# A streaming log-softmax backward kernel: 128-row tiles in 32 KiB runs become 256-row groups with 64 KiB runs and a new store order

## The chip, the cores and the metric

The kernel runs on one core of a Trainium2 chip. The metric is the device time of one execution in microseconds (us), taken as the median over several executions. The executions were made on several chips. The kernel before was run beside each experiment, and its medians on four of these chips were 1871.6, 1871.72, 1871.8 and 1871.83 us. The chips therefore differ by about 0.2 us. A profile is of one execution; its trace holds the instructions and the DMA packets. The span of a profile is 1.7 to 2.0 us shorter than the time of the execution that it shows.

A DMA moves data between DRAM and SBUF, the core's working memory, which is laid out in 128 partitions. PSUM is a second memory of the core. 16 DMA engines share the work of each DMA in the profiles here. They move it as packets: a run of 32 KiB, that is 32 KiB that lie in one piece in both memories, is one packet. At the end of a DMA each engine leaves one small packet more, its completion record. A buffer is the space for one tile.

## The reference, cut to what matters

```python
# y, dy: float32 [8, 1024, 8192]
softmax_x = np.exp(y)
sum_dy = np.sum(dy, axis=-1, keepdims=True)
return dy - softmax_x * sum_dy          # float32
```

There are 8,192 rows of 8,192 numbers. The row sum needs all of a dy row before the first output of that row can be made. Two arrays are read and one is written, 268.4 MB each, 805.3 MB in all. No change to the kernel can lessen that.

## The kernel before

A tile holds 128 rows, one row (32 KiB) per partition. For each tile the kernel loads dy, loads y, sums dy on the vector engine (DVE), takes exp on the scalar engine (ACT) into PSUM, and computes dy - sum * exp in place on DVE, 2,048 columns at a time. Three tiles are computed and then stored together. All DMAs are issued from the sync engine's queue (SP).

```python
def subtract_scaled_exp(nc, psum, y_part, dy_part, neg_sum, width):   # width = 2048
    for c in range(0, y_part.shape[-1], width):
        e_t = psum.tile([128, width], fp32)
        nc.scalar.activation(e_t[:], y_part[:, c : c + width], ACT_EXP)
        nc.vector.scalar_tensor_tensor(out=dy_part[:, c : c + width], in0=e_t[:],
            scalar=neg_sum, in1=dy_part[:, c : c + width], op0=ALU.mult, op1=ALU.add)
# dyp: BATCH + 1 = 4 buffers, yp: 2 buffers
for b, e in zip(starts, starts[1:] + [n_tiles]):          # BATCH = 3 tiles
    done = []
    for i in range(b, e):
        sl = ts(i, P)
        nc.sync.dma_start(out=dy_t[:], in_=dy_f[sl])       # [128, 8192]
        nc.sync.dma_start(out=y_t[:], in_=y_f[sl])
        nc.vector.tensor_reduce(out=s_t[:], in_=dy_t[:], axis=X, op=ALU.add, negate=True)
        subtract_scaled_exp(nc, psum, y_t, dy_t, s_t[:], CD)
        done.append((sl, dy_t))
    for sl, dy_t in done:
        nc.sync.dma_start(out=out_f[sl], in_=dy_t[:])
# ... allocation lines cut
```

## Time and profile before

| | kernel before |
|---|---|
| time, median | 1871.77 us (3 runs, 1871.63 to 1871.79) |
| span of the profile | 1870.2 us |
| bytes moved, mean rate | 805 MB, 431 GB/s |
| DVE, ACT busy | 61%, 26% |

The first excerpt is from the page of the kernel before: busy time per engine, the share of busy DMA in 40 slices of the span, the rate in the same slices, the packets, the DMA queue, the chain that ended last, and the three costly groups of instructions (busy us, mean ns of one, then the engine's idle time in front of them and what ended it).

```profile
DVE 1136.0 (61%) x320; ACT 477.5 (26%) x257; POOL 0.2 (0%) x4
...
DMA  9999999999999999999999999999999999999998
GB/s 404 437 428 435 429 435 431 433 435 429 435 430 435 432 432 435 429 435 430 434 434 430 436 429 433 433 432 435 431 433 432 432 435 430 435 430 434 434 432 383
DMA packets 27656, 805.38 MB, mean 431 GB/s; under 512 B 3072, under 2 KB 3072, under 8 KB 3072
...
q1 hardware_dynamic: 27648, 805.32, 100.0%
...
DMA 61%; DVE 13%; ACT 5%; SPq 1%; issue 0%; DVEq 0%; ACTq 0%
...
L69 DVE TENSOR_REDUCE s_t<-dy_t 128x1 f32<-128x8192 f32 x64 | 555.4, 8679 | 576.0 <-DMA dy_t<-in_dy_dram 576.0
L19 ACT ACTIVATE e_t<-y_t 128x2048 f32<-128x2048 f32 x256 | 476.3, 1877 | 1370.6 <-DMA y_t<-in_y_dram 1295.5
L20 DVE SCALAR_TENSOR_TENSOR dy_t<-e_t,s_t,dy_t 128x2048 f32<-128x2048 f32 x256 | 584.0, 2344 | 139.5 <-ACT e_t L19 139.5
```

Read it from the DMA rows. The 16 DMA engines are busy in every slice, and their queue fills 100.0% of the span. The compute engines wait for loads. The chain that ended last gives DVE 13% and ACT 5%, but this only says who waited for whom at each step; a gain on DVE would come to nothing while the DMA stays full. 3,072 of the 27,656 packets are completion records (16 per DMA, 192 DMAs) and 24,576 are 32 KiB each.

### The profile page before, as it was taken

The numbers are of one execution on the slowest core, as the hardware profiler recorded it, in microseconds if no ns is written. First come the engines' busy times: TensorE is split into PE (matmuls) and PEld (weight loads), VectorE is DVE, ScalarE is ACT, GpSimd is POOL, SyncE is SP. The second block draws the span as 40 slices with busy tenths as digits, with TensorE's granted clock in tenths as the row PEclk, the third lists the DMA queues.
The fourth block names the chain that finished last, engine by engine and source line by source line (L and its number), as shares of the span: only waits on it lengthen the run. The fifth ranks groups of instructions, "written<-read, shape, count | busy, mean of one in ns | idle before, by whom it ended". The sixth has DMA issues, their size and how long they took to land.

```text
span 1870.2 us, 1067 instructions
## 1 busy us (share of the span) xinstructions
DVE 1136.0 (61%) x320; ACT 477.5 (26%) x257; POOL 0.2 (0%) x4
## 2 busy tenths in 40 slices
DVE  6738384756657383839384755647383839374655
ACT  2214131313223131314131313223131414131322
POOL 0000000000000000000000000000000000000000
DMA  9999999999999999999999999999999999999998
GB/s 404 437 428 435 429 435 431 433 435 429 435 430 435 432 432 435 429 435 430 434 434 430 436 429 433 433 432 435 431 433 432 432 435 430 435 430 434 434 432 383
DMA packets 27656, 805.38 MB, mean 431 GB/s; under 512 B 3072, under 2 KB 3072, under 8 KB 3072
## 3 DMA queue, kind: packets, MB, share of 16 engines
q1 hardware_dynamic: 27648, 805.32, 100.0%
q14 instruction: 8, 0.07, 0.0%
HBM read 536.87 MB, written 268.44 MB: 431 GB/s over the span
## 4 chain that ended last, share of the span: by engine, by line
DMA 61%; DVE 13%; ACT 5%; SPq 1%; issue 0%; DVEq 0%; ACTq 0%
DMA y_t<-in_y_dram 61%; DVE dy_t L20 13%; ACT e_t L19 5%; SPq L65 1%; SPq L75 0%; DVEq L101 0%; ACTq L19 0%; SPq L67 0%
## 5 line engine op out<-in xcount | busy, mean ns | idle before, releaser
L69 DVE TENSOR_REDUCE s_t<-dy_t 128x1 f32<-128x8192 f32 x64 | 555.4, 8679 | 576.0 <-DMA dy_t<-in_dy_dram 576.0
L19 ACT ACTIVATE e_t<-y_t 128x2048 f32<-128x2048 f32 x256 | 476.3, 1877 | 1370.6 <-DMA y_t<-in_y_dram 1295.5
L20 DVE SCALAR_TENSOR_TENSOR dy_t<-e_t,s_t,dy_t 128x2048 f32<-128x2048 f32 x256 | 584.0, 2344 | 139.5 <-ACT e_t L19 139.5
L19 ACT ACT_TABLE_LOAD x1 | 1.3, 1283 | 0.7 <-PEq L90 0.7
L90 POOL MEMSET const-bfloat16-1.0<- 128x1 bf16 x1 | 0.1, 102 | 0.0
L90 POOL MEMSET const-uint8-127<- 128x1 uint8 x1 | 0.1, 102 | 0.0
L90 POOL MEMSET const-float32-0.0<- 128x1 f32 x1 | 0.1, 99 | 0.2 <-issue 0.2
L90 POOL MEMSET const-float32-1.0<- 128x1 f32 x1 | 0.1, 99 | 0.0
## 6 DMA issues: line engine op xcount, KB each, us to landing
dy_t<-in_dy_dram SPq DMA_DIRECT2D x64, 4096.0 KB, 45.2
y_t<-in_y_dram SPq DMA_DIRECT2D x64, 4096.0 KB, 36.3
out_dram<-dy_t SPq DMA_DIRECT2D x64, 4096.0 KB, 27.7
```

Source lines behind the costliest of these rows:

```text
L19: nc.scalar.activation(e_t[:], y_part[:, c : c + width], ACT_EXP)
L20: nc.vector.scalar_tensor_tensor(out=dy_part[:, c : c + width], in0=e_t[:], scalar=neg_sum, in1=dy_part[:, c : c + width], op0=ALU.mult, o ...
L65: nc.sync.dma_start(out=dy_t[:], in_=dy_f[sl])
L69: nc.vector.tensor_reduce(out=s_t[:], in_=dy_t[:], axis=mybir.AxisListType.X, op=ALU.add, negate=True)
L90: nc = _bacc.Bacc("TRN2", target_bir_lowering=False, num_devices=1)
```

## The change: its intent and its diff

A group is now 256 rows with two neighbouring rows per partition. For dy and out these two rows are contiguous in DRAM and in SBUF, so a run is 64 KiB long instead of 32. y stays at 32 KiB. Two 64 KiB y buffers beside two of dy would take 256 KiB in each partition, where the tiles of both kernels take 192. The number of DMAs falls from 192 to 129. exp now overwrites y in SBUF (no PSUM), 4,096 columns at a time. Each store is queued behind the dy load of the following group, and the last store but one is held back behind the last y loads.

```diff
-    CD = 2048
-    BATCH = 3
+    R = 2
+    G = N // (P * R)
+    CD = D // 2
+    dy_v = dy.flatten_outer_dims().rearrange("(g p r) d -> g p (r d)", p=P, r=R)   # y, out alike
-    dyp = ... bufs=BATCH + 1      yp = ... bufs=2      psum = ... bufs=2
+    dyp = ... bufs=2              yp = ... bufs=R
+    def load_dy(g):
+        dy_t = dyp.tile([P, R * D], fp32, name="dy_t")
+        nc.sync.dma_start(out=dy_t[:], in_=dy_v[g])
+        nc.vector.tensor_reduce(out=s_t[:], in_=dy_t[:].rearrange("p (r d) -> p r d", r=R), ...)
+    def load_y(g):                    # R loads of one row per partition
+        nc.sync.dma_start(out=y_t[:], in_=y_v[g][:, r * D : (r + 1) * D])
+    def compute(dy_t, s_t, y_ts):     # for r in range(R), for c in range(0, D, CD)
+                nc.scalar.activation(e, e, EXP)
+                nc.vector.scalar_tensor_tensor(out=d, in0=e, scalar=s_t[:, r : r + 1], in1=d, ...)
+    cur = load_dy(0)
+    for g in range(G):
+        if g < G - 1:
+            y_ts = load_y(g)
+            compute(*cur, y_ts)
+            nxt = load_dy(g + 1)
+            if g < G - 2:
+                store(g, cur[0])
+                cur = nxt
+            else:
+                held, cur = cur, nxt
+        else:
+            y_ts = load_y(g)
+            compute(*cur, y_ts)
+            store(g - 1, held[0])
+            store(g, cur[0], parts=R)
# ... cut: the removed helper and loop shown above, the body of store()
```

More of the change, by code (lines that the diff above doesn't have):

```diff
@@ L7 @@
 from concourse.bass import ts
-ACT_EXP = mybir.ActivationFunctionType.Exp
+EXP = mybir.ActivationFunctionType.Exp
 ALU = mybir.AluOpType
-def subtract_scaled_exp(nc, psum, y_part, dy_part, neg_sum, width):
-    total = y_part.shape[-1]
-    for c in range(0, total, width):
-        e_t = psum.tile([128, width], mybir.dt.float32, name="e_t")
-        nc.scalar.activation(e_t[:], y_part[:, c : c + width], ACT_EXP)
-        nc.vector.scalar_tensor_tensor(
-            out=dy_part[:, c : c + width],
-            in0=e_t[:],
-            scalar=neg_sum,
-            in1=dy_part[:, c : c + width],
-            op0=ALU.mult,
-            op1=ALU.add,
-        )
 @with_exitstack
@@ L42 @@
     fp32 = mybir.dt.float32
-    y_f = y.flatten_outer_dims()
-    dy_f = dy.flatten_outer_dims()
-    out_f = out.flatten_outer_dims()
-    N, D = y_f.shape
-    n_tiles = N // P
-    assert N == n_tiles * P
-    CD = 2048
-    BATCH = 3
-    dyp = ctx.enter_context(tc.tile_pool(name="dyp", bufs=BATCH + 1))
-    yp = ctx.enter_context(tc.tile_pool(name="yp", bufs=2))
-    psum = ctx.enter_context(tc.tile_pool(name="psum", bufs=2, space=bass.MemoryType.PSUM))
-    stats = ctx.enter_context(tc.tile_pool(name="stats", bufs=8))
@@ L58 @@
-    first = n_tiles % BATCH
-    starts = [0] * bool(first) + list(range(first, n_tiles, BATCH))
-    for b, e in zip(starts, starts[1:] + [n_tiles]):
-        done = []
-        for i in range(b, e):
-            sl = ts(i, P)
-            dy_t = dyp.tile([P, D], fp32, name="dy_t")
-            nc.sync.dma_start(out=dy_t[:], in_=dy_f[sl])
-            y_t = yp.tile([P, D], fp32, name="y_t")
-            nc.sync.dma_start(out=y_t[:], in_=y_f[sl])
-            s_t = stats.tile([P, 1], fp32, name="s_t")
-            nc.vector.tensor_reduce(
-                out=s_t[:], in_=dy_t[:], axis=mybir.AxisListType.X, op=ALU.add, negate=True
-            )
-            subtract_scaled_exp(nc, psum, y_t, dy_t, s_t[:], CD)
-            done.append((sl, dy_t))
-        for sl, dy_t in done:
-            nc.sync.dma_start(out=out_f[sl], in_=dy_t[:])
+    N, D = y.flatten_outer_dims().shape
@@ new lines @@
+    R = 2
+    G = N // (P * R)
+    assert N == G * P * R
+    CD = D // 2
+    y_v = y.flatten_outer_dims().rearrange("(g p r) d -> g p (r d)", p=P, r=R)
+    dy_v = dy.flatten_outer_dims().rearrange("(g p r) d -> g p (r d)", p=P, r=R)
+    out_v = out.flatten_outer_dims().rearrange("(g p r) d -> g p (r d)", p=P, r=R)
+    dyp = ctx.enter_context(tc.tile_pool(name="dyp", bufs=2))
+    yp = ctx.enter_context(tc.tile_pool(name="yp", bufs=R))
+    stats = ctx.enter_context(tc.tile_pool(name="stats", bufs=2))
@@ new lines, in load_dy @@
+    def load_dy(g):
+        dy_t = dyp.tile([P, R * D], fp32, name="dy_t")
+        nc.sync.dma_start(out=dy_t[:], in_=dy_v[g])
+        s_t = stats.tile([P, R], fp32, name="s_t")
+        nc.vector.tensor_reduce(
+            out=s_t[:],
+            in_=dy_t[:].rearrange("p (r d) -> p r d", r=R),
+            axis=mybir.AxisListType.X,
+            op=ALU.add,
+            negate=True,
+        )
+        return dy_t, s_t
+    def load_y(g):
+        y_ts = []
+        for r in range(R):
+            y_t = yp.tile([P, D], fp32, name="y_t")
+            nc.sync.dma_start(out=y_t[:], in_=y_v[g][:, r * D : (r + 1) * D])
+            y_ts.append(y_t)
+        return y_ts
@@ new lines, in compute, with store @@
+    def compute(dy_t, s_t, y_ts):
+        for r in range(R):
+            for c in range(0, D, CD):
+                e = y_ts[r][:, c : c + CD]
+                d = dy_t[:, r * D + c : r * D + c + CD]
+                nc.scalar.activation(e, e, EXP)
+                nc.vector.scalar_tensor_tensor(
+                    out=d, in0=e, scalar=s_t[:, r : r + 1], in1=d, op0=ALU.mult, op1=ALU.add
+                )
+    def store(g, dy_t, parts=1):
+        w = R * D // parts
+        for k in range(parts):
+            nc.sync.dma_start(
+                out=out_v[g][:, k * w : (k + 1) * w], in_=dy_t[:, k * w : (k + 1) * w]
+            )
```

## The prediction

> **What bounds the kernel now.** The page of the kernel before shows the DMA engines at nine tenths or more in nearly every slice; one queue takes 100.0% of the 16 engines' span, 805 MB at 431 GB/s. DVE is busy 61%, ACT 26%. The chain that ended last names y loads (61%). The trace's packet records say what the DMA time is made of: 24,576 packets of 32 KiB, 1,213 ns at the median; all packets over 16 engines make 1,867.7 us of the 1,870.2 us span (1,215.9 ns each, 1,536 an engine). There is almost no DMA idle time to win; only the cost per byte or packet can fall.
>
> **What the change does to that.** The bytes stay. The Trainium skill, page "DMA: Bandwidth & Descriptors", section "Where 436 GB/s comes from", gives 16 x 32 B x 850 MHz = 435.2 GB/s as ceiling: 1,204.7 ns for 32 KiB, 1,850.5 us for all. The trace agrees within 1%: 1,213 ns, 8 to 11 ns per packet over it. I estimate that this excess is fixed per packet. dy and out go to 64 KiB packets, y stays: 1,024 packets an engine. 512 x 8 to 11 ns saves 4 to 6 us. If the excess is per byte, or 64 KiB runs are split, nothing. Fewer completions (129 DMAs, not 192; 9 ns a record): under 1 us.
>
> **What moves.** Per 256-row group the DMA has about 58 us (three transfers of 19.4). DVE needs two row sums (8.68 us each now) and four scaled adds of 4,096 (2.28 us per 2,048 now, so about 4.5 each): 35 us. ACT: 14. Both fit. Critical is the store: behind the last y half[...] come an exp of 4,096 (3.6 us), two scaled adds (9), issue and first byte (1.7): about 16 us. The next dy load, queued in front of that store, feeds the DMA for 19.4 us: 3 us of slack, no bubble. The dy load after that waits for the older store to complete, but has two y loads (19.4 us) in front. y buffers are now freed by DVE, not ACT (exp in place), yet their loads sit behind the store that waits for the same work: nothing lost. At the start, dy, row sums and adds take about 58 us against 60 us of queued loads: 0 to 1.5 us lost. At the end the last compute hides under the held-back store; the tail stays.
>
> **Prediction.** 1871.8 - 4.5 + 0.5, rounded: 1867.5 us, range 1860 to 1875. Faster by over 2%: 0.01 (the ceiling is 1.1% away). Within 2%: 0.94. Slower by over 2%: 0.05.
>
> **What would show it.** About 18,600 DMA packets, not 27,656; a 64 KiB packet near 2,418 to 2,424 ns; 432 to 433 GB/s; no slice under 425 except first and last; DVE and ACT busy nearly as before (1,136 and 470 us); in the DMA queue's waits, stores waiting for scaled adds while the DMA stays full.
>
> **What would make it wrong.** Packets split, nothing gained (1872). The 3 us of slack eaten by slower SBUF operands or by DMA engines that drift apart: then each of 32 groups gets a bubble, and 1 us each costs 32 us. y rows 64 KiB apart meeting a slower HBM pattern, seen as 32 KiB packets over 1,213 ns.

One clause is cut from it: a figure of 2 us for the landing of data after its last packet. No trace shows it; those of the two kernels show 0.3 to 0.5 us.

## The result, and the profile after

The changed kernel took 1867.83 us (median of 6 runs, 1867.19 to 1872.63) against 1871.68 us (median of 6). The ratio of its runs to those of the kernel before is 0.9986, with a 95% interval of 0.9973 to 0.9999: the same within 2%, but just clear of 1. A ratio here is the mean time of one kernel's runs over that of the other's in the same rounds, so it is not quite the ratio of the medians. The prediction was 1867.5 us.

The same parts of the page for the changed kernel:

```profile
DVE 1119.2 (60%) x160; ACT 457.1 (25%) x129; POOL 0.2 (0%) x4
...
DMA  9999999999999999999999999999999999999999
GB/s 427 416 434 431 443 433 422 435 437 436 427 433 431 440 430 434 431 429 441 433 437 425 433 442 431 434 425 436 438 434 433 428 434 437 437 431 430 429 435 396
DMA packets 18582, 805.36 MB, mean 432 GB/s; under 512 B 2064, under 2 KB 2064, under 8 KB 2064
...
q1 hardware_dynamic: 18576, 805.31, 99.9%
...
DMA 74%; DVE 17%; ACT 6%; SPq 1%; issue 1%; DVEq 0%; ACTq 0%
...
L70 DVE SCALAR_TENSOR_TENSOR dy_t<-y_t,s_t,dy_t 128x4096 f32<-128x4096 f32 x128 | 568.1, 4481 | 490.3 <-ACT y_t L69 490.1
L69 ACT ACTIVATE y_t<-y_t 128x4096 f32<-128x4096 f32 x128 | 455.9, 3608 | 1375.6 <-DMA y_t<-in_y_dram 1375.6
L47 DVE TENSOR_REDUCE s_t<-dy_t 128x2 f32<-128x16384 f32 x32 | 551.0, 17220 | 232.1 <-DMA dy_t<-in_dy_dram 232.1
```

The DMA is still full; there are a third fewer packets. Nothing else that matters has moved. The DVE wait in front of the scaled adds grew from 139.5 to 490.3 us at no cost, because DVE is not the bottleneck. In the DMA queue's own waits, the stores wait for the scaled adds, as predicted, for 985.9 us in all, while the DMA stays full:

```profile
SPq L77 <- DVE dy_t L70: 985.9, 32, 35.0
```

The slices of the rate jump more than before (416 to 443) because the view books a packet's bytes in the slice in which it starts. With the bytes spread evenly over each packet's duration, all slices but the first and the last lie between 430 and 434 GB/s.

Next is the timeline of the changed kernel for one group (start us, duration us, instruction, and the idle time before it), which shows the store order at work.

```profile
149.38 7.12 ACT L69 ACTIVATE y_t<-y_t 128x4096 f32<-128x4096 f32 x2 [41.51 <-DMA y_t<-in_y_dram]
...
159.10 7.12 ACT L69 ACTIVATE y_t<-y_t 128x4096 f32<-128x4096 f32 x2 [2.59 <-DMA y_t<-in_y_dram]
162.75 8.88 DVE L70 SCALAR_TENSOR_TENSOR dy_t<-y_t,s_t,dy_t 128x4096 f32<-128x4096 f32 x2 [0.83 <-ACT y_t L69]
171.66 0.34 SPq L77 DMA_DIRECT2D out_dram<-dy_t  x1
172.09 0.86 SPq L60 DMA_DIRECT2D y_t<-in_y_dram  x2
178.45 17.22 DVE L47 TENSOR_REDUCE s_t<-dy_t 128x2 f32<-128x16384 f32 x1 [6.83 <-DMA dy_t<-in_dy_dram]
```

The second y half's last packet ended at 158.62 us (from the packet records), and exp began at 159.10: the data counted as landed 0.5 us after its last packet. The store was issued at 171.66. The first DMA of the kernel was issued at 0.73 and its first packet is at 1.74, so a store's first packet can start about 1 us after its issue, here at about 172.7. The 16 engines do not finish the dy load in front of it together: the first is done at 176.97 and the last at 178.06. The store was ready about 5.3 us before the last engine needed it, but only 4.3 us before the first did. This margin is called the slack below.

The packet records of the traces say where the 4.8 us between the two spans went. (The two profiled executions took 1872.19 and 1867.19 us, 5.0 us apart, where the medians are 3.9 us apart. So up to about 1 us of what follows may belong to these two executions and not to the kernels.) In this table "sum" is the duration of all packet records over 16 engines. "Overlap" is the time in which more than 16 records were open, over 16: an engine opens the next record a little before the last one closes. (The records do not name their engine. They can be chained into 16 rows by letting each record follow one that it overlaps by a few ns; within such a row the overlap is 3.5 ns a record.) "Mean finish" and "last finish" are the ends of the 16 engines' last completion records. "Slow" is what packets over 30 ns above their median took beyond it, over 16. All are us, finishes from the start of the span.

```
kernel      packets   median ns of    sum      overlap  mean    last    slow
            an engine 32 KiB  64 KiB                    finish  finish
before        1536    1213      -     1869.39    6.06   1865.48 1868.97  1.89
changed       1032    1213    2418    1864.28    4.14   1862.16 1864.20  2.57
difference    -504                      -5.11   -1.92     -3.32   -4.77
```

A 64 KiB packet takes 2,418 ns where two of 32 KiB took 2,426. The 504 packets saved per engine take 504 x 8 = 4.0 us out of the records, 63 fewer completions of 9 ns about 0.6 us, and small items the rest of the 5.1 us. But 1.9 us of that had been overlapped before and was no time at all. What is left, 3.2 us, is what the mean finish shows (3.3 us). The last 1.4 us are at the end: in the kernel before, the slowest engine finished 3.5 us behind the mean, in the changed one 2.0 us.

### The profile page after: what moved, and what is told of

Same layout as the page of the kernel before. It is cut to its first block, busy times and chain, and to the rows that moved or that the text cites. A ratio compares the mean times of both kernels' runs of the same rounds, so it can differ in the third digit from the quotient of the medians. Undisturbed runs are those within 1.5% of the kernel's fastest.

```text
span 1865.4 us, 712 instructions
## 1 busy us (share of the span) xinstructions
DVE 1119.2 (60%) x160; ACT 457.1 (25%) x129; POOL 0.2 (0%) x4
## 2 busy tenths in 40 slices
DMA packets 18582, 805.36 MB, mean 432 GB/s; under 512 B 2064, under 2 KB 2064, under 8 KB 2064
## 4 chain that ended last, share of the span: by engine, by line
DMA 74%; DVE 17%; ACT 6%; SPq 1%; issue 1%; DVEq 0%; ACTq 0%
DMA y_t<-in_y_dram 69%; DVE dy_t L70 15%; ACT y_t L69 6%; DMA dy_t<-in_dy_dram 3%; DVE s_t L47 2%; DMA out_dram<-dy_t 1%; SPq L60 1%; SPq L77 1%; DVEq L122 0%; ACTq L69 0%; DVEq L70 0%
## 5 line engine op out<-in xcount | busy, mean ns | idle before, releaser
L70 DVE SCALAR_TENSOR_TENSOR dy_t<-y_t,s_t,dy_t 128x4096 f32<-128x4096 f32 x128 | 568.1, 4481 | 490.3 <-ACT y_t L69 490.1
L69 ACT ACTIVATE y_t<-y_t 128x4096 f32<-128x4096 f32 x128 | 455.9, 3608 | 1375.6 <-DMA y_t<-in_y_dram 1375.6
L47 DVE TENSOR_REDUCE s_t<-dy_t 128x2 f32<-128x16384 f32 x32 | 551.0, 17220 | 232.1 <-DMA dy_t<-in_dy_dram 232.1
```

The source lines that it names most:

```text
L47: nc.vector.tensor_reduce(out=s_t[:], in_=dy_t[:].rearrange("p (r d) -> p r d", r=R), axis=mybir.AxisListType.X, op=ALU.add, negate=True,)
L69: nc.scalar.activation(e, e, EXP)
L70: nc.vector.scalar_tensor_tensor(out=d, in0=e, scalar=s_t[:, r : r + 1], in1=d, op0=ALU.mult, op1=ALU.add)
```

## The experiments

Theory A, the prediction's: each packet carries a fixed cost of about 8 ns whatever its size, so longer runs of bytes are the gain, and the rest (order of stores, exp in place) only has to keep the DMA fed. Rival B: the gain is from fewer DMAs or from spreading the stores, not from run length. Rival C: the cost is per byte and the gain is chance. All edits are to the changed kernel; all results were correct.

### The changed kernel unedited, as the baseline

> The changed kernel, unedited, as the baseline on this chip. All theories: about 1867.5 us, 3 to 5 us under the kernel before. The first six runs ranged from 1867.2 to 1872.6, so single runs near 1872 may come again; their share is what this run is also for.

Measured: 1867.3 us (5 runs, 1866.79 to 1871.63), ratio 0.9982 (0.9969 to 0.9994). The gain repeats. One execution of five was at 1871.63 us.

### 32 KiB packets with the same DMAs

```diff
-        dy_t = dyp.tile([P, R * D], fp32, name="dy_t")
-        nc.sync.dma_start(out=dy_t[:], in_=dy_v[g])
+        dy_t = dyp.tile([P, R, D + 16], fp32, name="dy_t")
+        nc.sync.dma_start(out=dy_t[:, :, :D], in_=dy_v[g].rearrange("p (r d) -> p r d", r=R))
# row sums, adds and stores address dy_t[:, r, ...] accordingly
```

> Same DMAs, same order, same sizes as the changed kernel, but a 64-byte gap between the two rows in SBUF forces 32 KiB packets. Theory A (a fixed cost of about 8 ns per packet): 1,544 packets an engine instead of 1,032, packets back at 1,213 ns, so +4 us: about 1871.5 us, level with the kernel before. Rival B (the gain comes from fewer DMAs or from the new order of stores): stays at about 1867.5 us. Rival C (per-byte cost, gain from fewer slow packets by luck): no clear difference from the changed kernel.

Measured: 1871.32 us (1869.19 to 1876.59, 5 runs), ratio to the kernel before 1.0003 (0.999 to 1.0015). This line of its page shows the packets (24,576 of 32 KiB and, as in the changed kernel, 2,064 completions in 129 DMAs, besides 6 of the instruction queue):

```profile
DMA packets 26646, 805.36 MB, mean 430 GB/s; under 512 B 2064, under 2 KB 2064, under 8 KB 2064
```

The number of DMAs, their order and their bytes are those of the changed kernel, and the gain is gone. That speaks for A and against B. The five executions scatter, though (1869.19 to 1876.59 us), so the next experiment was needed.

### 32 KiB packets by one DMA per row

```diff
-        nc.sync.dma_start(out=dy_t[:], in_=dy_v[g])
+        for r in range(R):
+            nc.sync.dma_start(out=dy_t[:, r * D : (r + 1) * D], in_=dy_v[g][:, r * D : (r + 1) * D])
-    def store(g, dy_t, parts=1):
+    def store(g, dy_t, parts=R):
```

> The changed kernel with dy and out moved as two 4 MiB DMAs each, one per row of the pair: 32 KiB packets and 192 DMAs, as many as before, in the new order. Theory A: about 1871.5 to 1872 us; against the padded variant only 63 more completions, under 1 us. Rival B, number of DMAs: clearly slower than the padded variant. Rival B, order of stores: about 1867.5 us.

Measured: 1871.29 us (1870.82 to 1871.86, 5 runs), ratio to the kernel before 0.9999 (0.9986 to 1.0011). With the new order, exp in place and large groups, but with the old packets and the old number of DMAs, the kernel is level with the one before. Its page has the packets of the kernel before:

```profile
DMA packets 27655, 805.38 MB, mean 431 GB/s; under 512 B 3072, under 2 KB 3072, under 8 KB 3072
```

The intervals of the two ratios overlap, so the difference rests on the single executions: 13 of 16 of the changed kernel, over its three sets, lie between 1866.79 and 1868.23 us, and all five of this one between 1870.82 and 1871.86. It is also level with the padded variant, so 63 completions more or less do not show in the medians. The length of the runs of bytes carries the gain.

### 16 KiB and 8 KiB packets

```diff
-        dy_t = dyp.tile([P, R * D], fp32, name="dy_t")
+        dy_t = dyp.tile([P, R * S, W + 16], fp32, name="dy_t")     # S = 2 or 4, W = D // S
-            y_t = yp.tile([P, D], fp32, name="y_t")
+            y_t = yp.tile([P, S, W + 16], fp32, name="y_t")
```

> All three tensors in 16 KiB packets, same DMAs and order as the changed kernel: 3,072 packets an engine. Theory A: 2,040 more packets an engine at 8 ns is +16 us, about 1884 us, with packets of about 611 ns at the median. Per-byte rival: unchanged, about 1868 us, packets of 606 ns.

> All three tensors in 8 KiB packets: 6,144 an engine. Theory A: 5,100 more packets an engine than the changed kernel at 8 ns is +41 us, about 1908 us, packets of about 309 ns. Per-byte rival: about 1868 us.

Measured: 1876.7 us (1876.27 to 1877.53, 4 runs) and 1893.73 us (1893.14 to 1894.08, 4 runs). Both are slower, so the per-byte rival C is out. But the size is a miss: +9.4 and +26.4 us over the changed kernel where 8 ns a packet gave +16 and +41. The packet records explain it:

```
kernel      packets   median ns   sum      overlap  mean    last
            an engine one packet                    finish  finish
one DMA/row   1536      1213     1869.22    6.06   1865.21 1868.81
16 KiB        3072       611     1881.69   12.30   1871.85 1873.62
8 KiB         6144       309     1906.21   20.17   1888.47 1890.57
```

The records' excess did behave as expected (611 and 309 ns). The overlap grows along with the number of packets, at 3.3 to 4.0 ns each, and that part is never paid. In mean finish, with 9 ns per completion taken off, a further packet costs (1871.85 - 1865.21 + 0.57) / 1536 = 4.7 ns from 32 to 16 KiB, 5.4 ns from 16 to 8 KiB, and (1865.21 - 1861.85 - 0.57) / 504 = 5.5 ns from 64 to 32 KiB (1861.85 us is the baseline run's mean finish). These are differences of single profiles, and they depend on which ones are taken. The padded variants start their first packet 0.4 us later, which makes the first figure 4.4 ns. The padded 32 KiB variant would give 9.3 ns for the last step with the same correction, but its profiled execution (1873.6 us, above its median) had 2.7 us more of slow packets than the baseline's; without these it gives 4.0. Taken from the medians of the executions instead, with the end of the kernel in them, the three steps are 3.9, 5.5 and 6.8 ns. So a fixed cost is real at all these sizes, and about 5 ns by the records' mean finish; the 8 ns of the records alone are not what a packet costs. At 16 and 8 KiB no run separates the padding from the packet size; at 32 KiB the padded variant and the one without padding are level. The Trainium skill, page "DMA: Bandwidth & Descriptors", section "Why small descriptors are slow (HBM only)", speaks of a fixed overhead of about 3 cycles per packet. If these are cycles of the 850 MHz in its neighbouring section, which the page does not say, an estimate is 3.5 ns. The runs here show about 5 ns (4.4 to 5.5), the same order, and show it at packets of up to 64 KiB, where the page's example is 256 bytes. That it is the same overhead is not shown.

### How much slack the store order leaves

```diff
# at the end of compute(), after the group's last scaled add; n = 1 or 3
+        for _ in range(n):
+            nc.vector.tensor_scalar(out=d, in0=d, scalar1=1.0, scalar2=None, op0=ALU.mult)
```

> One more pass over the last 4,096 columns (times 1.0, about 2.2 us on the vector engine) before each group's store. The trace of the changed kernel puts the store's first packet about 5 us before the end of the dy load queued in front of it (the prediction said 3). Both figures: the delay fits in the slack, no change, about 1867.5 us. If the DMA queue has no real slack: 31 x 2.2 = +68 us.

> Three such passes, about 6.6 us per group. Slack of 5.2 us, as read from the trace: a bubble of about 1.4 us in each of 31 groups, about 1910 us. Slack of 3 us, as predicted: 3.6 us each, about 1980 us. If the slack is far larger than read: no change.

Measured: 1879.11 us (1876.3 to 1880.64, 5 runs) with one pass and 1952.19 us (1952.0 to 1952.43, 4 runs) with three. Both numbers are misses: no change and about 1910 us were expected. (They are compared with the 1867.3 us of the changed kernel on another chip; on this one only the kernel before was run beside them, at 1871.72 us.) The timelines of the two, one pass first, show one group each:

```profile
396.75 8.88 DVE L70 SCALAR_TENSOR_TENSOR dy_t<-y_t,s_t,dy_t 128x4096 f32<-128x4096 f32 x2 [0.83 <-ACT y_t L69]
405.67 2.29 DVE L74 TENSOR_SCALAR dy_t<-dy_t 128x4096 f32<-128x4096 f32 x1
407.99 0.34 SPq L79 DMA_DIRECT2D out_dram<-dy_t  x1
...
412.40 17.22 DVE L47 TENSOR_REDUCE s_t<-dy_t 128x2 f32<-128x16384 f32 x1 [4.43 <-DMA dy_t<-in_dy_dram]
```

```profile
361.86 6.95 DVE L74 TENSOR_SCALAR dy_t<-dy_t 128x4096 f32<-128x4096 f32 x3
368.83 0.34 SPq L79 DMA_DIRECT2D out_dram<-dy_t  x1
369.27 1.34 SPq L60 DMA_DIRECT2D y_t<-in_y_dram  x2
369.38 17.22 DVE L47 TENSOR_REDUCE s_t<-dy_t 128x2 f32<-128x16384 f32 x1 [0.57 <-DMA dy_t<-in_dy_dram]
```

With three passes, 6.95 us are added, and the packet records have no packet at all open for 48.4 us, 1.56 us per group over 31 groups. 6.95 - 1.56 = 5.4 us: with the engines in step, as they are in this run, the slack is what the trace showed for the last engine. What the expectation lacked is the price of a queue that ran empty. Packets over 30 ns above their median took 29.4 us an engine in all, 27 us more than in the changed kernel, or 0.9 us per restart, and engines starting and stopping apart took the rest of the 85 us. These slow packets are mostly one per engine and group: the last packet of a store (23 of the 29.4 us).

With one pass the DMA as a whole was never empty before the end, though 14 of the 16 engines ran dry for up to 0.64 us each in front of the first store. Slow packets took 11.4 us instead of 2.6, 7.7 of them in the second half of the span, which is the 9 us by which that profiled execution was longer. The packet records of the 21st store (us after the store's issue) show both runs beside the changed kernel:

```
kernel        dy load in front of it ends    last packets of the     their mean excess
              first engine    last engine    store start             over 2,418 ns
changed           2.85            6.25       19.76 .. 23.15             0 ns
one pass          1.52            4.50       18.42 .. 21.40           267 ns
three passes     -1.18           -0.75       17.84 .. 18.00           754 ns
```

The engines drift apart. The completion records of one DMA lie 0.7 us apart at the start of the changed kernel and 3.4 us apart late in it. So the first engine's slack shrinks: the store's data can flow about 1 us after its issue, which leaves that engine 1.9 us at the 21st store, where the last one has 5.3. One pass of 2.3 us is more than 1.9. This fits the time lost before the 5.2 us read from the trace are used up, though with one pass the engines seldom ran dry: what cost the time was the slow packets.

It would be natural to blame the slow packets on engines in step, as they are after an empty queue. The traces do not bear this out. In the one-pass run the second to fourth stores end with all 16 engines within 0.9 us of one another, and the slow packets there are 0.02 us an engine or less; the 2,048-column variant below is as close together at the same stores and has none. What goes with the slow packets is the first engine's margin. Over the first 30 stores of six profiles (three of the changed kernel, the 2,048-column variant and the two delayed runs), the slow packets at a store's end were under 0.05 us an engine in all 130 stores where the first engine finished the dy load 2 us or more after the store's issue. They were 0.2 to 0.5 us in the last 16 of these stores of the one-pass run, where that time was 0.7 to 1.6 us, also in those where the engines were 2 us and more apart. This is something that goes together in the traces; no run was made to separate it. Why the loss falls on the last packet of the store, some 20 us later, stays open.

### y in 64 KiB packets too

```diff
-    yp = ctx.enter_context(tc.tile_pool(name="yp", bufs=R))
+    yp = ctx.enter_context(tc.tile_pool(name="yp", bufs=1))
+        y_t = yp.tile([P, R * D], fp32, name="y_t")
+        nc.sync.dma_start(out=y_t[:], in_=y_v[g])          # one load per group
```

> y as well in 64 KiB packets: one 8 MiB load per group into one buffer. Theory A: 256 fewer packets an engine, 2 us less packet time, 64 KiB packets at 2,418 ns. But the chain behind the y landing grows to 0.5 + 3.6 + 17.7 + 1.0 = 22.8 us against 19.35 us of dy load in front of the store: about 3.5 us of bubble in 31 groups, so about 1970 to 1975 us.

Measured: 2004.43 us (2 runs). There are 256 packets an engine fewer, but the chain behind the y landing no longer fits under the dy load: no packet is open for 102.2 us, 3.3 us per group (3.5 expected), and slow packets take another 27 us, as in the delayed run. This is why the change leaves y at 32 KiB. The expectation was short by the cost of the restarts.

### The store in front of the dy load: a first attempt that did not do it

```diff
-            nxt = load_dy(g + 1)
-            if g < G - 2: ...          # and the held-back store at the end
+            store(g, cur[0])
+            cur = load_dy(g + 1)
```

> One part undone: each store is queued in front of the next group's dy load (all 64 KiB runs stay). If the order is what keeps the DMA fed, the queue now blocks on the scaled adds with nothing behind the y load: from the last y packet to the first store packet about 17 us per group (dy landing, 17.2 us of row sums, 17.7 us of adds, 1 us of issue, less 19.4 us of y load), about 2410 us. If the order doesn't matter: 1867.5 us.

Measured: 1876.03 us (2 runs, 1873.93 and 1878.12), which would say that the order hardly matters. The timeline tells otherwise:

```profile
346.16 0.34 SPq L77 DMA_DIRECT2D out_dram<-dy_t  x1
346.59 0.86 SPq L60 DMA_DIRECT2D y_t<-in_y_dram  x2
...
372.58 0.33 SPq L45 DMA_DIRECT2D dy_t<-in_dy_dram  x1
...
404.58 0.34 SPq L77 DMA_DIRECT2D out_dram<-dy_t  x1
```

The dy load is still issued before the store, although the program now names it after. The scheduler of the compiler kept it there; that it did so because the load is ready sooner is likely but not shown. Only the end of the queue differs from the changed kernel, where the last store but one is no longer held back. So this run is a test of that alone: the last compute has nothing to hide under, the DMA is empty for 4.3 us, and the span is 6.8 us longer (1872.2 against 1865.4).

### The store in front of the dy load, by an ordering edge

```diff
+            s = store(g, cur[0])
+            with tc.issue_after(s.ins):      # issue order only, no wait for completion
+                cur = load_dy(g + 1)
# and each y load is kept behind the DMAs that were issued before it
```

> The store now really queued in front of the next group's dy load, by an ordering edge (the first attempt only moved the last store, because the scheduler kept the old order elsewhere). From the end of a group's y packets to the store's first packet: dy landing 0.5, row sums 17.2, adds 17.7, issue 1.0, less 19.4 of y load: about 17 us, plus about 1 us for restarting an empty queue as the delayed runs showed: 18 us x 32 = +575 us, about 2440 us. If the order does not matter: 1867 us.

Measured: 2434.49 us (2 runs). The page's DMA rows, and the timeline of one group:

```profile
DMA  6977769777797777977769777797777977779778
...
q1 hardware_dynamic: 18576, 805.31, 77.7%
```

```profile
344.65 17.67 DVE L71 SCALAR_TENSOR_TENSOR dy_t<-y_t,s_t,dy_t 128x4096 f32<-128x4096 f32 x4
...
362.35 0.34 SPq L78 DMA_DIRECT2D out_dram<-dy_t  x1
362.74 0.42 SPq L45 DMA_DIRECT2D dy_t<-in_dy_dram  x1
```

The DMA is empty for 532 us, 16.6 us per group, as computed (17), and the packets of its restarts cost 26 us. The changed kernel has two dy buffers, and the order of its stores is what makes two enough. That order keeps the DMA full; it does not by itself make it faster, as the one-DMA-per-row run showed.

### 2,048 columns at a time, for a version better than both

```diff
-    CD = D // 2
+    CD = D // 4
```

> exp and scaled add on 2,048 columns at a time instead of 4,096: the chain behind the last y landing shrinks by about 1.7 us, so the store is queued about 7 us before the dy load ends, not 5. If the DMA is the only bound, the median stays at about 1867.3 us; if the changed kernel's runs at 1871 to 1872 come from a store queued too late (slow turnaround packets), they should become rarer and the slow packets fewer.

> The changed kernel once more, beside the 2,048-column variant on the same chip, for the spread of its runs: median about 1867.5 us, one run in four or five near 1871 to 1872 us.

Measured: 1868.66 us (1867.34 to 1869.61, 5 runs) and, for the changed kernel beside it, 1867.7 us (1867.28 to 1868.23, 5 runs). More slack brings nothing. The changed kernel had no execution over 1870 us here, so this pair says nothing of the rare longer ones: 3 of the changed kernel's 16 timed executions in all lay between 1871 and 1873 us, and their cause stays open, since no profile fell on one. The pair also settles exp in place. exp of 2,048 took 1,877 ns into PSUM and 1,897 ns into SBUF, the scaled add 2,344 ns from PSUM and 2,347 ns from SBUF.

No version beat the changed kernel. With all bytes in 64 KiB packets an engine would have 256 packets fewer, about 1.3 us at 5 ns each (an estimate from the cost above); that is what an arrangement with room for y could still gain by run length.

## Why the prediction was right, point by point

- **Total.** 1867.5 us predicted, 1867.83, 1867.3 and 1867.7 us measured in three sets of runs. Right. The range given, 1860 to 1875, also held the 1872 us of "nothing gained", so the range by itself tests little; the packet experiments do.
- **What bounds the kernel.** The DMA, with no idle time to win. Right: when the packets were put back to 32 KiB, all else new, the time was back (ratio 0.9999).
- **A fixed cost per packet, 64 KiB runs not split.** Right in kind: a 64 KiB packet takes 2,418 ns (2,418 to 2,424 predicted), and there are 18,582 packets (18,600). The size was off. "512 x 8 to 11 ns saves 4 to 6 us" took the records' excess for time. Neighbouring records overlap by 3 to 4 ns, so a packet costs about 5 ns by the mean finish, and 504 x 5 is about 2.5 us.
- **What filled the rest.** About 0.6 us from fewer completions (under 1 us was predicted), and 1.4 us because the slowest engine finished closer to the mean. The prediction had said "the tail stays". This distance was 2.0 to 2.7 us in three profiles of the changed kernel, 3.5 before, 3.6 and 3.8 in the two 32 KiB variants, but 4.2 in the 2,048-column variant with the same packets as the changed kernel, so it is not a plain matter of packet size. It is how far the engines have drifted apart by the end; what sets that was not found. The right total thus rests partly on luck: the packets gave about 2 us less than forecast, and the end, the completions and a start without the 0.5 us of loss that was allowed for gave about as much more.
- **The store order keeps the DMA fed.** Right: the forced other order costs 567 us. With the engines in step the slack was 5.2 to 5.4 us, not 3; the prediction took 2 us for landing and 1.7 us for issue and first byte, and the trace shows 0.5 and 1.0. What it named only as a risk, engines that drift apart, takes most of this back: late in the kernel the first engine has 1.9 us.
- **A bubble of 1 us per group costs 32 us.** Too low: 1.56 us of empty DMA per group cost 85 us in all, 2.7 us per group. And time is lost before the 5.2 us are used up: 2.3 us already cost 12 us, which fits the 1.9 us of the first engine.
- **The start loses 0 to 1.5 us.** The first store was issued at 57.77 us and the dy load in front of it landed at 61.83 us, so nothing was lost there.
- **The sign "no slice under 425".** Wrong: two slices show 416 and 422 GB/s with a full DMA, because of how packets are booked.
- **What would have made it wrong.** None of it came: 64 KiB runs were not split, no bubble opened, and y packets stayed at 1,213 ns with rows 64 KiB apart.

## What to carry to other kernels

When the DMA is full and the bytes are fixed, the number of packets is still a lever, but from 32 KiB runs on it was worth about 5 ns per packet and engine: two per mille here, so make sure first that the DMA is really full. Queue a store that waits for compute behind a load that does not. Read the slack for the DMA engine that finishes first, late in the kernel, and not for the last one: the engines drifted 3.4 us apart here, and an emptied queue cost about 1 us more than its gap. Check the order of issues in the trace before you believe an experiment on order, for the scheduler may have kept the old one.

## What the Trainium skill lacked or had wrong

- "DMA: Bandwidth & Descriptors", section "Where 436 GB/s comes from": its ceiling of 435.2 GB/s needs no mending. By an estimate from it, 64 KiB take 2,409.4 ns on one of 16 engines; the runs show 2,418 ns by the record and a mean of 432 GB/s over the whole span, within 1%.
- "DMA: Bandwidth & Descriptors", section "Why small descriptors are slow (HBM only)": it does not say that the cost per packet goes on at large runs. Here it is about 5 ns per packet between 8 and 64 KiB.
- The same page, section "Anatomy of one DMA": its fixed cost of about 2 us is for the GpSimd path, and section "Latency and other measured facts" gives about 0.6 us to the first byte for the sync queue. The runs show 1.0 us from the start of the issuing instruction to the first packet, but 0.6 us from its end, so the two agree if the page counts from there, which it does not say. From the last packet to the first instruction that uses the data the runs show 0.3 to 0.5 us, for which the page has no figure on the sync queue.
- No page read tells what an emptied queue costs at its restart: about 0.9 us in slow packets per engine and restart, besides the gap (in the run with three passes, most of it in the last packet of the store).
- No page read says that packet records overlap, by 3 to 4 ns each here, so that their durations must not be added up as time.
- No page read says how far the 16 engines drift apart in a long stream: the completions of one DMA came to lie 3.4 us apart in the changed kernel, and the slack of the engine in front fell from 4.3 us (third store) to 1.9 us (21st store).
